# Neighbourhood attention in a hybrid encoder: full-height score passes, equal key chunks, V split once by key columns, heads' output split during the gates

## The chip, the cores and the metric

The kernel runs on one core of one Trainium2 chip. The metric is the device time of one execution in microseconds (us). Of the core's engines, PE is TensorE (PEld its weight loads), DVE is VectorE, ACT is ScalarE, POOL is GpSimd, and SP is SyncE, which here issues most DMAs.

## What is computed

One encoder layer on two sequences with shared weights: a sample of 512 tokens and a prompt of 1024, each with 16 meta tokens in front.

```
h = rmsnorm(x) * g_mix
q, k, v, u, gate_na, gate_fn = split(h @ w_in)
y_na = neighbourhood_attention(q, k, v) @ w_branch_na     # 8 heads of 64
y_fn = fourier_mix(u) @ w_branch_fn
x = x + (sigmoid(gate_na) * y_na + sigmoid(gate_fn) * y_fn) @ w_out
x = x + relu(rmsnorm(x) * g_mlp @ w_up) ** 2 @ w_down
```

and a final rmsnorm. The tokens form a grid of 64 columns. Each attends to 8 rows x 16 columns of the grid around it, with a bias by relative position, and to all meta tokens.

## The kernel before

Every float32 operand of a product is split into two parts of 12 bits, hi and lo, and hi.hi, hi.lo and lo.hi are summed in PSUM: three passes of PE. A split is an ACT copy (hi) and a subtraction (lo), on DVE out of PSUM (`split_ps`, L113) and on POOL out of SBUF (`split_sb`, L131, used by `weights`, L124). Weights stream through three kinds of tiles with two buffers each: raw, hi and lo.

The sequences go one after the other, the sample first. For each, `run` (L312) computes V (`project_v`, L274), then the attention (L429), the gates (L690), the product of the heads' output with its branch weights (`merge_na`, L712), the Fourier branch, the output projection and the MLP. A planner orders each engine's instructions by the trace of the program, by priority and by what is ready in its own model, so loads can be issued well ahead of their place in the program; what `behind` (L99) encloses stays behind marks on its engines. In a queue an instruction that waits holds up those after it.

**V.** A tile of 128 tokens is 24 matmuls, a DVE copy, and one DMA of 256 KB to a place `vd` in DRAM (L305). `spread_v` (L647) then copies V from DRAM to DRAM into the order of the key chunks, `vf` (L660), and the rests of chunks to `vp` (L674). For each head and block of query rows, `values` (L499) loads V from there and splits it: ACT L512 and POOL L513, for rests L519 and L520.

**Units.** A unit is 128 queries of a head: 8 rows by 16 columns of the grid. Four units (j = 0 to 3, for 24, 32, 32 and 24 key columns) make a block of 8 query rows; the sample has one such block for each head, the prompt two. So the sample has 32 units and the prompt 64. A unit has three stages:

- the scores: the queries' hi and lo stand in the two halves of a tile of 128 rows, and the keys' hi in both halves, so one pass (L549) gives hi.hi and lo.hi. A second one (L550) gives hi.lo from the 64 rows of the head. The bias is loaded by SP (L686). DVE adds it and takes the least (L554), ACT takes the exponential (L556), DVE the reciprocal (L557) and the product (L558).
- the transposes of the probabilities (L564), chunk by chunk, each split by ACT and DVE (L115, L116). A chunk is a whole number of key rows: 120, 128 or 96 keys, and in some blocks of 32 key columns a rest of 32 keys, which has splits of its own.
- the products with V (L585), two for each chunk, of 128 and 64 output columns.

After j = 3, ACT copies half of the sum (L589), DVE adds it to the other (L590), and ACT and POOL split the result into `oT` in SBUF (L593, L594), in the order of the tokens.

The stages of different units overlap by lags (L613). Between them PE gets steps of three matmuls (L444 to L446): the queries and keys of the next pair of heads (`project`, L450), early gates (L596), and in the sample a folding of weights (L217). The steps are dealt out so that they are used up after 5/6 of the units of a pair:

```
nxt = chain(project(pr + 1) if pr < 3 else after, islice(early, 8 * quota[pr]))
...
step(x, lambda s: feed(min(steps, (3 * u + s + 1) * steps * 6 // (3 * nu * 5))))
```

**Gates.** For each of eight blocks of 128 channels, one or two weight tiles of 512 KB are loaded, and 24 matmuls for each 512 tokens follow. Gates that were computed early come back from DRAM first (L695).

Of the kernel before, what the change touches and what calls it, by code (L numbers as in the profile page):

```python
# [33 lines left out]
KC0 = (0, 8, 24, 40)  # L34
QC, KCOL, VC, GNA, GFN = 0, 512, 1024, 2048, 3072
# [6 lines left out]
def row_blocks(rows):  # L42
    """How a block of 8 query rows meets its keys, for column blocks with 24 and with 32 key columns.

    Key slots: the meta tokens, the key rows, the meta tokens again. s0, n: first slot and number of
    slots; rpc, full: slots to a chunk and number of full chunks; meta: where the meta tokens are;
    row0: where key row 0 of the loads is; loads: (table, first of 8 reversed query rows, how many,
    first key row, how many, offset); masked: (first query, last, first slot, last) never loaded."""
    if rows == 8:
        loads = [("un", 0, 8, 0, 8, 7)]  # L50
        return [{24: dict(s0=0, n=10, rpc=5, full=2, meta=0, row0=1, loads=loads, masked=[(0, 128, 9, 10)]),
                 32: dict(s0=0, n=9, rpc=4, full=2, meta=0, row0=1, loads=loads, masked=[])}]
    first = [("un", 4, 4, 0, 8, 7), ("4", 0, 4, 0, 11, 7)]
    last = [("4", 4, 4, 0, 12, 3), ("un", 0, 4, 4, 8, 3)]
    b0 = dict(s0=0, n=12, rpc=4, full=3, meta=0, row0=1, loads=first, masked=[(64, 128, 9, 12)])
    return [{24: b0, 32: b0},
            {24: dict(s0=3, n=15, rpc=5, full=3, meta=14, row0=2, loads=last, masked=[(0, 128, 0, 2), (0, 64, 2, 6)]),
             32: dict(s0=5, n=13, rpc=4, full=3, meta=12, row0=0, loads=last, masked=[(0, 64, 0, 4)])}]


class Layer:
# [27 lines left out]
    def mark(self):  # L89
        """The last instruction so far of each engine that the weights pass."""  # L90
# [22 lines left out]
    def split_ps(self, ps, hi, lo, ref=None):  # L113
        """hi + lo = ps, exactly. ref: where hi is read, if not where it is written."""
# [3 lines left out]
    def wtile(self, kind, shape):  # L118
        """A tile of up to 1044 columns of the pool through which the weights stream."""
# [4 lines left out]
    def weights(self, src, to=None, scale=1.0, lo_engine=None):  # L124
        """One weight tile: DMA, then the exact split. to: the pair of tiles for it, if not of the streaming pool."""
# [25 lines left out]
    def norm(self, x, gain, out, n=128, junk=None):  # L151
        """out = rmsnorm(x) * gain for n tokens, one to a partition."""
# [5 lines left out]
        # y = (2 v) ** -0.5: a first guess, negative, from the bits, then Newton steps, each of which turns the sign  # L158
# [9 lines left out]
    def transpose_in(self, hn, hT, pos, n=128):  # L168
        """hT[:, kt, pos:pos+n] (hi and lo) = hn[:n].T, where hT is in one pair of tiles or in more"""
# [13 lines left out]
    def tables(self):  # L183
        """Tables of negated biases in DRAM: "un" has the column mask, "4" the row mask as well.

        The queries of a block lie in reverse order (last row first, last column first), so that
        the tables are read with positive strides."""
        nc, tc = self.nc, self.tc
        self.g = {(t, w): self.dram.tile([2, 16 * H, 15 * w], F32, name=f"g_{t}{w}") for t in ("un", "4") for w in (24, 32)}
        # negated meta biases, between masked columns  # L190
# [4 lines left out]
        with tc.tile_pool(name="tab", bufs=1, side="right", reuse_waits="tile") as p:  # L195
# [5 lines left out]
            for w in (24, 32):  # L201
                # blocks (0, 3) or (1, 2)
# [14 lines left out]
    def fold_u(self, p):  # L217
        """W_u times the channel DFT of its group: columns [256 cos | 4 nyquist | 252 sin], hi and lo, to DRAM."""
# [871 lines left out]
```

## Time and profile before

| | before |
|---|---|
| median of 3 runs (lowest to highest) | 2160.71 us (2157.1 to 2161.77) |
| span of the profiled execution | 2160.5 us |
| mean granted clock of PE | 0.984 |
| PE idle for DVE, ACT, POOL or DMA, longest single wait | 8.2 us, for DVE L166, at the start |

The profile is of one execution. Its span reaches from the first to the last instruction. A row of the timeline has the start (us from the span's start), the duration, the engine, the line of the kernel, the operation, the tile written, the tiles read, the shape, and how many instructions are merged in it. In brackets stands for how long the engine was idle before, and what ended that. Rows of the chain have start, length and what ran. Rows of a window have its length and then the busy time of each engine, the granted clock (1.00 is full), the mean busy share of the DMA engines and what they moved in GB/s.

### The profile page before, as it was taken

To read this page: it belongs to the slowest core of one execution; us is meant where nothing else is said; L and a number is where in the kernel's file an instruction comes from. 1 tells how busy PE (TensorE), PEld (TensorE's weight loads), DVE (VectorE), ACT (ScalarE), POOL (GpSimd) and SP (SyncE) were. 2 spreads that over 40 slices of the span, in tenths; PEclk is the share of its full clock that TensorE was granted. 3 is DMA by queue.
4 is the path that set the end of the run, shared out by engine and by line. 5 is a ranking of instruction groups with operands and counts; after the bars stand their busy time and mean duration, and the time that the engine had idled before them with its cause. 6 is when DMAs were issued, how large, how long until landed. Compare 5 with 4: busy or idle time off the path is not lost.

```text
span 2160.5 us, 26214 instructions
## 1 busy us (share of the span) xinstructions
PE 2100.4 (97%) x9947; PEld 1710.0 (79%) x9947; DVE 1072.0 (50%) x1937; ACT 699.4 (32%) x1321; POOL 700.7 (32%) x644
## 2 busy tenths in 40 slices
PE   6999999999999999999999999999999999999998
PEld 4877877878888788777788788788888888888886
DVE  6571155565664544565500627275445544454446
ACT  3673322433332315566532213132122112211221
POOL 3343545244444412444413624203122112221120
PEclk9999989999999999999989999999999999999999
DMA  6644543334323344333422253302112111121111
GB/s 201 192 143 152 141 132 100 92 108 126 114 82 103 110 158 148 102 101 85 127 78 59 60 162 105 136 10 78 39 49 62 46 40 45 54 59 39 39 40 78
DMA packets 232090, 205.01 MB, mean 95 GB/s; under 512 B 39982, under 2 KB 202542, under 8 KB 231790
## 3 DMA queue, kind: packets, MB, share of 16 engines
q1 hardware_dynamic: 219196, 187.97, 28.8%
q0 software_dynamic: 12768, 15.37, 2.9%
q8 instruction: 78, 1.28, 0.3%
q14 instruction: 48, 0.39, 0.1%
HBM read 184.29 MB, written 27.38 MB: 98 GB/s over the span
## 4 chain that ended last, share of the span: by engine, by line
PE 84%; DVE 8%; DMA 2%; issue 2%; ACT 2%; POOL 1%; POOLq 0%; SPq 0%; DVEq 0%; ACTq 0%
PE ps_o L111 23%; PE ps_s L111 23%; PE ps_mm L111 23%; PE ps_mm L444 3%; PE ps_mm L445 3%; PE ps_mm L446 3%; PE ps_o L585 2%; PE ps_t L564 1%; PE ps_s L550 1%; DVE s L756 1%; PE ps_t L176 1%; DVE hn L783 1%; DVE hn L166 1%; PE ps_s L549 1%; POOL hT L759 0%
## 5 line engine op out<-in xcount | busy, mean ns | idle before, releaser
L135 POOL TENSOR_TENSOR w_lo<-w_raw,w_hi 128x1024 fp32r<-128x1024 f32 x175 | 422.1, 2416 | 991.1 <-ACT w_hi L134 468.9
L957 DVE TENSOR_TENSOR relu<-relu 128x512 f32<-128x512 f32 (+1 forms) x98 | 204.1, 2083 | 357.9 <-ACT relu L956 357.9
L134 ACT CAST w_hi<-w_raw 128x1024 fp32r<-128x1024 f32 x176 | 182.9, 1048 | 361.2 <-DMA w_raw<-in_w_up 93.9
L444 PE MATMUL ps_mm<-hT,w_hi 128*128 128x512 f32 (+3 forms) x304 | 125.3, 412 | 1.7 <-DVE wu_lo L116 1.7
L111 PE MATMUL ps_s<-gate,w_hi 128*128 128x512 f32 (+1 forms) x528 | 126.9, 390 | 0.0
L111 PE MATMUL ps_mm<-gate,w_hi 128*128 128x512 f32 (+1 forms) x528 | 126.3, 388 | 0.2
L958 ACT CAST hid_hi<-relu 128x512 fp32r<-128x512 f32 (+1 forms) x98 | 60.0, 612 | 198.1 <-DVE relu L957 197.8
L111 PE MATMUL ps_o<-gate,w_hi 128*128 128x512 f32 (+1 forms) x512 | 122.8, 390 | 0.6 <-DVE gate L116 0.6
L111 PEld LDWEIGHTS ps_mm<-gate,w_hi 128*128 128x128 f32 x528 | 97.6, 188 | 23.1 <-DVE gate L116 0.8
L111 PEld LDWEIGHTS ps_s<-gate,w_hi 128*128 128x128 f32 x528 | 98.2, 188 | 22.2
L111 PEld LDWEIGHTS ps_o<-gate,w_hi 128*128 128x128 f32 x512 | 95.3, 188 | 22.8 <-DVE gate L116 0.9
L445 PE MATMUL ps_mm<-hT,w_hi 128*128 128x512 f32 (+3 forms) x304 | 108.9, 358 | 0.0
L446 PE MATMUL ps_mm<-hT,w_lo 128*128 128x512 f32 (+3 forms) x304 | 108.8, 358 | 0.0
L756 DVE TENSOR_TENSOR s<-s,s 128x384 f32<-128x384 f32 (+2 forms) x34 | 25.2, 778 | 163.2 <-POOL s L753 101.1
L984 DVE TENSOR_TENSOR acc<-acc,ps_o 128x512 f32<-128x512 f32 x120 | 81.8, 682 | 28.4 <-PE ps_o L111 28.4
L111 PE MATMUL ps_mm<-w_hi,hid_hi 128*128 128x512 f32 x240 | 94.0, 392 | 0.9 <-DVE acc L984 0.9
L959 DVE TENSOR_TENSOR hid_lo<-relu,hid_hi 128x512 fp32r<-128x512 f32 (+1 forms) x98 | 70.4, 718 | 48.0 <-ACT hid_hi L958 46.3
L984 DVE TENSOR_TENSOR acc<-acc,ps_s 128x512 f32<-128x512 f32 x120 | 81.8, 682 | 24.7 <-PE ps_s L111 24.7
L111 PE MATMUL ps_mm<-w_lo,hid_hi 128*128 128x512 f32 x240 | 93.5, 390 | 0.3 <-POOL w_lo L135 0.3
L984 DVE TENSOR_TENSOR acc<-acc,ps_mm 128x512 f32<-128x512 f32 x120 | 81.8, 682 | 24.2 <-PE ps_mm L111 24.1
L111 PE MATMUL ps_s<-w_hi,hid_hi 128*128 128x512 f32 x240 | 93.8, 391 | 0.0
L111 PE MATMUL ps_o<-w_hi,hid_hi 128*128 128x512 f32 x240 | 93.7, 391 | 0.0
(393 smaller groups left out, 4575.1 us busy)
## 6 DMA issues: line engine op xcount, KB each, us to landing
w_raw<-in_w_up SPq DMA_DIRECT2D x64, 512.0 KB
w_raw<-in_w_down SPq DMA_DIRECT2D x64, 512.0 KB
w_raw<-in_w_in SPq DMA_DIRECT2D x56, 512.0 KB
w_raw<-in_w_out SPq DMA_DIRECT2D x16, 512.0 KB
raw<-in_w_na SPq DMA_DIRECT2D x16, 256.0 KB
raw<-in_w_fnA SPq DMA_DIRECT2D x16, 256.0 KB
raw<-in_w_fnB SPq DMA_DIRECT2D x16, 256.0 KB
r<-in_x_prompt SPq DMA_DIRECT2D x8, 512.0 KB
```

The source lines that it names most:

```text
L111: self.nc.tensor.matmul(out, a, b, start=(i == 0), stop=(i == len(terms) - 1))
L134: nc.scalar.copy(out=hi, in_=raw)
L135: (lo_engine or nc.gpsimd).tensor_tensor(out=lo, in0=raw, in1=hi.bitcast(F32), op=ALU.subtract)
L444: nc.tensor.matmul(ps, a[0], b[0], start=(kt == 0), stop=False)
L445: nc.tensor.matmul(ps, a[0], b[1], start=False, stop=False)
L446: nc.tensor.matmul(ps, a[1], b[0], start=False, stop=(kt == 7))
L585: nc.tensor.matmul(po[:m, j * 128:(j + 1) * 128], v, x, start=(i == 0), stop=(i == len(ops) - 1))
L756: nc.vector.tensor_tensor(out=f[2 + i], in0=f[0], in1=f[1], op=(ALU.add, ALU.subtract)[i])
L957: nc.vector.tensor_tensor(out=r, in0=r, in1=r, op=ALU.mult)
L958: nc.scalar.copy(out=hi[:, cs], in_=r)
L959: nc.vector.tensor_tensor(out=lo[:, cs], in0=r, in1=hi[:, cs].bitcast(F32), op=ALU.subtract)
L984: nc.vector.tensor_tensor(out=acc[t][:, cs], in0=acc[t][:, cs], in1=ps, op=ALU.add)
```

## The change

- The lo of a head's keys is written to both halves of a tile of its own (`kl`, four buffers of one head instead of two of a pair). The second score pass goes over all 128 rows; it now adds lo.lo as well.
- A block's keys are the same slots for all its units: 9 slots in the sample, 12 and 13 in the prompt. They are cut into equal chunks: 2 x 108 and 3 x 96 keys in the sample, 3 x 96, 3 x 128, 3 x 104 and 4 x 104 in the prompt. No rests are left.
- V is split where it is computed, by ACT and DVE. Hi and lo go side by side to four places in DRAM, one for each block of key columns: eight DMAs for a tile of 128 tokens. `spread_v` goes. For each head and block of query rows, four DMAs bring hi and lo at once, in rows of 512 bytes, and nothing is split then.
- A head's output is put in the order of the tokens by DVE's addition and stored in DRAM (`od`). For each pair of heads it comes back through the weights' raw tiles and is split by ACT and POOL ahead of gate blocks 1 to 4. `oT` is allocated after the attention's pool is closed.

```diff
+KW = (24, 32, 32, 24)
+MPOS = (0, 16, 0, 8)
+VROW = H * 2 * DH
...
     if rows == 8:
-        loads = [("un", 0, 8, 0, 8, 7)]
-        return [{24: dict(s0=0, n=10, rpc=5, full=2, meta=0, row0=1, loads=loads, masked=[(0, 128, 9, 10)]),
-                 32: dict(s0=0, n=9, rpc=4, full=2, meta=0, row0=1, loads=loads, masked=[])}]
+        return [dict(s0=0, n=9, meta=0, row0=1, loads=[("un", 0, 8, 0, 8, 7)], masked=[])]
     first = [("un", 4, 4, 0, 8, 7), ("4", 0, 4, 0, 11, 7)]
     last = [("4", 4, 4, 0, 12, 3), ("un", 0, 4, 4, 8, 3)]
-    b0 = dict(s0=0, n=12, rpc=4, full=3, meta=0, row0=1, loads=first, masked=[(64, 128, 9, 12)])
-    return [{24: b0, 32: b0},
-            {24: dict(s0=3, n=15, rpc=5, full=3, meta=14, row0=2, loads=last, masked=[(0, 128, 0, 2), (0, 64, 2, 6)]),
-             32: dict(s0=5, n=13, rpc=4, full=3, meta=12, row0=0, loads=last, masked=[(0, 64, 0, 4)])}]
+    return [dict(s0=0, n=12, meta=0, row0=1, loads=first, masked=[(64, 128, 9, 12)]),
+            dict(s0=5, n=13, meta=12, row0=0, loads=last, masked=[(0, 64, 0, 4)])]
+def key_chunks(n):
+    c = -(-n // 128)
+    assert n % c == 0
+    return c, n // c
+def most_chunks(blocks):
+    return max(key_chunks(b["n"] * w)[0] for b in blocks for w in KW)
...
-        self.vd = self.dram.tile([128 + T, H, DH], F32, name=f"vd_{name}")
+        nslot = T // 64 + 2
+        most = most_chunks(row_blocks(T // 64))
+        self.vw = [self.dram.tile([nslot * w, VROW], F32, name=f"vw_{name}{j}") for j, w in enumerate(KW)]
         meta = self.meta_values
         if meta is not None:
-            for s in (0, 64 + T):
-                nc.sync.dma_start(self.vd[s:s + 64], meta)
-        self.meta_values = self.vd[0:64]
+            for j, w in enumerate(KW):
+                for s in (0, nslot - 1):
+                    nc.sync.dma_start(self.vw[j][s * w:(s + 1) * w], meta[j][0:w])
+        self.meta_values = self.vw
...
-            vs = p.tile([128, 512], F32R, name="pt0", tag="pt0", bufs=self.ptb).bitcast(F32)
-            nc.vector.tensor_copy(vs[:n], ps[:n])
-            vs = vs.rearrange("p (h d) -> p h d", h=H)
...
+            vs = p.tile([128, 4, most, 2 * DH], F32R, name="vb", tag="vb", bufs=2).rearrange("p j c x -> p (j c x)")
+            vs = vs[:, :VROW].rearrange("p (h i d) -> p h i d", h=H, i=2)
+            self.split_ps(ps[:n].rearrange("p (h d) -> p h d", h=H), vs[:n, :, 0], vs[:n, :, 1])
+            vs = vs.bitcast(F32).rearrange("p h i d -> p (h i d)")
+            for j, w in enumerate(KW):
+                if t < 0:
+                    at = self.vw[j][0, :]
+                    for m, c0 in ((16, MPOS[j]), (w - 16, 0 if MPOS[j] else 16)):
+                        nc.sync.dma_start(
+                            bass.AP(at.tensor, at.offset + c0 * VROW, [[VROW, m], [(nslot - 1) * w * VROW, 2], [1, VROW]]),
+                            vs[:m, None, :].to_broadcast([m, 2, VROW]))
+                else:
+                    for r in range(2):
+                        s = (1 + 2 * t + r) * w
+                        nc.sync.dma_start(self.vw[j][s:s + w], vs[r * 64 + KC0[j]:r * 64 + KC0[j] + w])
...
-            op, close_oT = self.open(f"oT_{name}", "left")
             with ExitStack() as fold:
                 after = self.fold_u(fold.enter_context(pool("fold", "right"))) if i == 0 else iter(())
-                oT = self.attention(att, op, name, T, hT, w0, after)
+                od = self.attention(att, name, T, hT, w0, after)
             close_att()
+            op, close_oT = self.open(f"oT_{name}", "left")
+            oT = [self.pair(op, [128, T], f"oT{pr}", 1) for pr in range(4)]
...
-            near_end = self.gates(T, hT, mixed, sig)
+            near_end = self.gates(T, hT, mixed, sig, lambda pr: self.weights(od[pr], oT[pr]))
...
-        oT = [[op.tile([128, T], F32R, name=f"oT{pr}{i}") for i in range(2)] for pr in range(4)]
+        most = most_chunks(blocks)
+        wide = max(b["n"] * w for b in blocks for w in KW)
+        od = [self.dram.tile([128, T], F32, name=f"o_{name}{pr}") for pr in range(4)]
...
-            kl = p.tile([128, nslot, 64], F32R, name="kl", bufs=2)
+            kl = [p.tile([128, nslot, 64], F32R, name="kl", bufs=4) for _ in range(2)]
...
-                    for hp in (own, slice(64 - 64 * hh, 128 - 64 * hh)):
+                    for hp in both:
...
-                    nc.vector.tensor_tensor(out=flat[2][own, gs], in0=src[:, m:], in1=flat[hh][own, gs].bitcast(F32),
-                                            op=ALU.subtract)
-                    if m:
-                        nc.vector.tensor_tensor(out=copies(kl, own), in0=src[:, None, None, :m].to_broadcast([64, 2, 3, 16]),
-                                                in1=copies(kh[hh], own).bitcast(F32), op=ALU.subtract)
+                    for hp in both:
+                        nc.vector.tensor_tensor(out=flat[2 + hh][hp, gs], in0=src[:, m:], in1=flat[hh][own, gs].bitcast(F32),
+                                                op=ALU.subtract)
+                        if m:
+                            nc.vector.tensor_tensor(out=copies(kl[hh], hp), in0=src[:, None, None, :m].to_broadcast([64, 2, 3, 16]),
+                                                    in1=copies(kh[hh], own).bitcast(F32), op=ALU.subtract)
...
-            nf = max(blk[w]["full"] for w in (24, 32))
-            vb = p.tile([128, 2, 2, nf, 2, DH], F32R, name="vb", tag="vb", bufs=2)
...
+            b = blocks[R]
+            vb = p.tile([128, 4, most, 2 * DH], F32R, name="vb", tag="vb", bufs=2)
+            for j, w in enumerate(KW):
+                nch, ck = key_chunks(b["n"] * w)
+                at = self.vw[j][0, :]
+                nc.sync.dma_start(vb[:ck, j, :nch].bitcast(F32),
+                                  bass.AP(at.tensor, at.offset + b["s0"] * w * VROW + h * 2 * DH,
+                                          [[VROW, ck], [ck * VROW, nch], [1, 2 * DH]]))
+            return vb
...
-            w = 24 if j in (0, 3) else 32
-            b = blk[w]
-            n, rpc, full, ck = b["n"], b["rpc"], b["full"], b["rpc"] * w
+            w = KW[j]
+            b = blk
+            n = b["n"]
             W = n * w
+            nch, ck = key_chunks(W)
...
-            nc.tensor.matmul(ps[:, :W], qs[hh][own, qc], kl[own, kw[0], kw[1]], start=False, stop=True)
+            nc.tensor.matmul(ps[:, :W], qs[hh][:, qc], kl[hh][:, kw[0], kw[1]], start=False, stop=True)
...
-            nch = full + (1 if n > full * rpc else 0)
             for c in range(nch):
-                k0, k1 = c * ck, min((c + 1) * ck, W)
-                nc.tensor.transpose(tp[:k1 - k0, c * 128:(c + 1) * 128], sc[:, k0:k1], self.ident)
+                nc.tensor.transpose(tp[:ck, c * 128:(c + 1) * 128], sc[:, c * ck:(c + 1) * ck], self.ident)
             pt = [p.tile([128, 512], F32R, name=f"pt{i}", bufs=self.ptb) for i in range(2)]
-            nf = full * 128
-            self.split_ps(tp[:ck, :nf], pt[0][:ck, :nf], pt[1][:ck, :nf])
-            if nch > full:
-                self.split_ps(tp[:32, nf:nf + 128], pt[0][:32, nf:nf + 128], pt[1][:32, nf:nf + 128])
+            self.split_ps(tp[:ck, :nch * 128], pt[0][:ck, :nch * 128], pt[1][:ck, :nch * 128])
...
-                k = ck if c < full else 32
-                v = (vb[:ck, (w == 32), j // 2, c] if c < full else vp[:, j // 2]).rearrange("p i d -> p (i d)")
-                ops.append((128, v, pt[0][:k, cs]))
-                ops.append((64, v[:, :64], pt[1][:k, cs]))
+                v = vb[:ck, j, c]
+                ops.append((128, v, pt[0][:ck, cs]))
+                ops.append((64, v[:, :64], pt[1][:ck, cs]))
...
-                ot = p.tile([128, 512], F32, name="ot", tag="ot", bufs=1)[own]
-                nc.scalar.copy(out=ot, in_=po[64:])
-                nc.vector.tensor_tensor(out=ot, in0=po[:64], in1=ot, op=ALU.add)
-                hi, lo = (t[own, R * 512:(R + 1) * 512].rearrange("p (i j a) -> p j i a", j=4, a=16) for t in oT[pr])
-                ov = ot.rearrange("p (j i a) -> p j i a", j=4, a=16)[:, :, ::-1, ::-1]
-                nc.scalar.copy(out=hi, in_=ov)
-                nc.gpsimd.tensor_tensor(out=lo, in0=ov, in1=hi.bitcast(F32), op=ALU.subtract)
+                half = p.tile([128, 512], F32, name="ot", tag="ot", bufs=1)[own]
+                ot = p.tile([128, 512], F32, name="os", bufs=2)[own]
+                nc.scalar.copy(out=half, in_=po[64:])
+                nc.vector.tensor_tensor(out=ot.rearrange("p (i j a) -> p j i a", j=4, a=16)[:, :, ::-1, ::-1],
+                                        in0=po[:64].rearrange("p (j i a) -> p j i a", j=4, a=16),
+                                        in1=half.rearrange("p (j i a) -> p j i a", j=4, a=16), op=ALU.add)
+                nc.sync.dma_start(od[pr][own, R * 512:(R + 1) * 512], ot)
...
-        self.spread_v(name, blocks)
...
-    def spread_v(self, name, blocks):
-        nc = self.nc
-        self.vfull, self.vpart = {}, {}
...
+        *sigs, bring = sigs
...
         for dm in range(8):
+            if dm in (1, 2, 3, 4):
+                bring(dm - 1)
             for sig, c0 in zip(sigs, (GNA, GFN)):

```

More of the change, by code (lines that the diff above doesn't have):

```diff
@@ L427, in new_hT, with attention @@
         return [tuple(pool.tile([128, 8, T + extra], F32R, name=f"hT{i}") for i in range(2))]
-    def attention(self, p, op, name, T, hT, w0, after):
+    def attention(self, p, name, T, hT, w0, after):
         hT, = hT
@@ L471, in project @@
                 gs = slice(t0, t0 + cn - m)
-                flat = [t.rearrange("p s c -> p (s c)") for t in kh + [kl]]
+                flat = [t.rearrange("p s c -> p (s c)") for t in kh + kl]
                 for hh in range(2):
                     own = slice(64 * hh, 64 * hh + 64)
+                    both = own, slice(64 - 64 * hh, 128 - 64 * hh)
                     src = ps[own, :cn]
-                    for hp in (own, slice(64 - 64 * hh, 128 - 64 * hh)):
+                    for hp in both:
                         nc.scalar.copy(out=flat[hh][hp, gs], in_=src[:, m:])
@@ L541, in unit @@
             qs, kh, kl = state[pr]
-            own = slice(64 * hh, 64 * hh + 64)
-            bm = p.tile([128, 416], F32, name="bm", bufs=8 if T == 512 else 4)
+            bm = p.tile([128, wide], F32, name="bm", bufs=8 if T == 512 else 4)
             self.bias(bm, h, j, w, b)
@@ L573, in unit @@
             po = shared["o"]
[L574 removed]
+            vb = shared["v"]
             ops = []
```

60 lines of the change are left out of this document (3 added, 57 removed).

## The prediction

> **What bounds the kernel now.** I read the page first, then the busy times by stage, then the timeline of TensorE (PE), then the rows of its waits.
>
> ```profile
> PE 2100.4 (97%) x9947; PEld 1710.0 (79%) x9947; DVE 1072.0 (50%) x1937; ACT 699.4 (32%) x1321; POOL 700.7 (32%) x644
> PE 84%; DVE 8%; DMA 2%; issue 2%; ACT 2%; POOL 1%; POOLq 0%; SPq 0%; DVEq 0%; ACTq 0%
> ```
>
> PE is busy for 2100.4 of 2160.5 us and carries 84% of the chain that ended last. So the change is worth what it takes from PE's own time, plus or minus idle time. It works in the two attention stages:
>
> ```profile
> 70.00:177.70 107.70, 98.07 (x589) 79.02 (x589) 72.61 (x235) 74.68 (x225) 44.79 (x84) 0.96 0.49 141
> 811.00:1088.00 277.00, 274.92 (x1523) 220.78 (x1522) 152.52 (x403) 161.16 (x386) 106.50 (x218) 0.97 0.39 110
> ```
>
> (Columns: window, length, busy PE, PEld, DVE, ACT, POOL, clock, DMA share, GB/s.) In the prompt's attention PE idles 2 us of 277: time taken from PE there is gained. The sample's has 10 us of idle, and DVE and ACT are busy for 70% of it.
>
> The end of a matmul row is modelled, so I price a pass by the distance from its start to the start of the next. One unit (128 queries of a head) in the prompt:
>
> ```profile
> 950.39 0.62 PE L585 MATMUL ps_o<-pt,vb 120*128 120x128 f32 x6
> 950.85 0.45 PE L444 MATMUL ps_mm<-hT,w_hi 128*128 128x512 f32 x1
> 951.14 0.40 PE L445 MATMUL ps_mm<-hT,w_hi 128*128 128x512 f32 x1
> ...
> 951.60 0.29 PE L549 MATMUL ps_s<-kh,q 128*128 128x288 f32 x1
> 951.83 0.40 PE L550 MATMUL ps_s<-kl,q 64*128 64x288 f32 x1
> 952.15 0.50 PE L444 MATMUL ps_mm<-hT,w_hi 128*128 128x512 f32 x1
> 952.50 0.39 PE L445 MATMUL ps_mm<-hT,w_hi 128*128 128x512 f32 x1
> 952.73 0.39 PE L446 MATMUL ps_mm<-hT,w_lo 128*128 128x512 f32 x1
> ```
>
> and passes of full height among their like:
>
> ```profile
> 101.82 0.29 PE L444 MATMUL ps_mm<-hT,w_hi 128*128 128x264 f32 x1
> 101.94 0.28 PE L445 MATMUL ps_mm<-hT,w_hi 128*128 128x264 f32 x1
> 965.50 0.33 PE L445 MATMUL ps_mm<-hT,w_hi 128*128 128x352 f32 x1
> 965.67 0.32 PE L446 MATMUL ps_mm<-hT,w_lo 128*128 128x352 f32 x1
> ```
>
> **Term 1, the second score pass.** L549 to L550 takes 0.23 us, L550 to the next 0.32, and that one 0.35: 0.90. Among full-height passes 264 columns take 0.12 and 352 take 0.17, so 288 take 0.13; 512 take 0.23 (952.50 to 952.73). Two score passes and their follower without the 64-row neighbour: 0.13 + 0.13 + 0.23 = 0.49. The 64-row pass thus costs 0.41 a unit, on both its sides. The new pass has 128 rows (the keys' lo in both halves) and the same columns: 96 units x 0.41 = 39.4 us of PE. It could be nothing, if the place and not the height made these gaps (rival E), and not much more. The Trainium skill (TensorEngine Tiling (Array Packing), Key Properties) says that a change of tiling mode drains TensorE, which is this step; it gives no figure, and the trace agrees with the 0.23 and 0.32 above.
>
> **Term 2, the 32-row value passes.** Units with 32 key columns in the sample, and in the prompt's second row block, end with a short chunk:
>
> ```profile
> 87.06 0.45 PE L585 MATMUL ps_o<-pt,vb 128*128 128x128 f32 x4
> 87.44 0.38 PE L585 MATMUL ps_o<-pt,vp 32*64 32x128 f32 x2
> 87.75 0.50 PE L444 MATMUL ps_mm<-hT,w_hi 128*128 128x512 f32 x1
> 88.08 0.39 PE L445 MATMUL ps_mm<-hT,w_hi 128*128 128x512 f32 x1
> ```
>
> 0.38 + 0.31 + 0.33 = 1.02, where six even passes and their follower take 0.46 + 0.29 = 0.75 (950.39 to 951.14). Equal chunks (3 x 96; 4 x 104) keep the number of passes: 32 units x 0.27 = 8.6 us.
>
> **Term 3, columns.** Blocks of 24 key columns lose 24 columns in the sample (240 to 216) and 48 in the prompt's second block (360 to 312): 16 units each, two passes, at 0.05 us for 88 columns: 1.3 us. Sum of the three: 49 us.
>
> **What of it lands.** From 5/6 of each pair's units on (L640) no projection lies between the units. There DVE's loop of reduce, wait for ACT's exponential, reciprocal, multiply sets the pace:
>
> ```profile
> 961.23 0.58 DVE L554 CUSTOM_DVE_ANT_0 sc<-ps_s,bm 128x416 f32<-128x416 f32 x1
> 963.18 0.58 DVE L554 CUSTOM_DVE_ANT_0 sc<-ps_s,bm 128x416 f32<-128x416 f32 x1
> 965.12 0.53 DVE L554 CUSTOM_DVE_ANT_0 sc<-ps_s,bm 128x360 f32<-128x360 f32 x1
> ```
>
> 1.95 us a unit. By 1/6 these are 16 of 96 units; I count their gain, 0.41 and a third of 0.27, half: 4 us are lost (bounds 0 and 8). In the sample PE falls from 98.07 by 13.1 + 4.3 + 0.3 to about 80, near DVE's 72.61; I take 3 us lost (0 to 8).
>
> **V.** The splits that go were these, on ACT and POOL:
>
> ```profile
> L512 ACT CAST vb<-vr x48: 399/510/518, 75.8 to 1069.1; 128x384 fp32r<-128x384 f32 x16, 120x256 fp32r<-120x256 f32 x8, 128x256 fp32r<-128x256 f32 x8, 96x384 fp32r<-96x384 f32 x8
> L513 POOL TENSOR_TENSOR vb<-vr,vb x48: 724/1008/1119, 76.3 to 1071.0; 128x384 fp32r<-128x384 f32 x16, 120x256 fp32r<-120x256 f32 x8, 128x256 fp32r<-128x256 f32 x8, 96x384 fp32r<-96x384 f32 x8
> ```
>
> 24 us of ACT and 48 of POOL, beside PE except once:
>
> ```profile
> 60.88 9.16 DMA vf_sample<-vd_sample
> 70.09 5.72 DMA vr<-vf_sample
> 75.83 0.41 ACT vb L512
> 77.42 0.76 PE L564 MATMUL ps_t<-ident,sc 128*128 128x128 f32 x3 [1.39 <-DVE sc L558]
> 77.40:82.00 4.60, 4.58 (x17) 3.75 (x18) 2.71 (x11) 4.25 (x15) 1.95 (x5) 0.63 0.79 200
> ```
>
> V's copies between DRAM places end at 70.0, its load at 75.8, and ACT stands at V's split with the first exponential behind it. PE idles 1.39 us, and the next 4.6 us go at a mean clock of 0.63, which costs 4.6 x 0.37 = 1.7 us. Afterwards no ACT work waits for V, and nothing copies it between DRAM places: a gain of 3 us (0 to 3). V's loads, issued where the old one was (70.1), are first used four units later (L613), some 10 us, against the 5.72 above.
>
> What is added: each tile of V (24 matmuls of 0.23: 5.5 us of PE) is split by ACT and DVE and stored by eight DMAs instead of one. On SP the row below prices the issue, so 3 us a tile: it fits, with the score biases queued behind it, which have four or eight buffers. The lo of the keys is written twice: DVE again, 40 x 0.5 and 16 x 0.25, is 24 us over both stages, beside PE; the separate splits of short chunks go from DVE.
>
> ```profile
> L305 SPq DMA_DIRECT2D vd_prompt<-pt x8: 320/379/571, 779.2 to 816.1; - x8
> L480 DVE TENSOR_TENSOR kl<-ps_mm,kh x34: 401/500/520, 63.8 to 989.7; 64x344 fp32r<-64x344 f32 x12, 64x264 fp32r<-64x264 f32 x8, 64x336 fp32r<-64x336 f32 x8, 64x248 fp32r<-64x248 f32 x6
> 1069.74 0.38 SPq L128 DMA_DIRECT2D w_raw<-in_w_in  x1
> ...
> 1072.09 20.86 SPq L695 DMA_DIRECT2D gate<-gate_prompt x6
> ```
>
> **The heads' output.** The new store of a head's block waits on SP for DVE, with biases and, at the end of attention, the gates' loads behind it. SP already stands for 20.86 us at that place, up to 1093, five us past the end of attention (1088), and the first weights had been issued ahead of it (1069.74). Four loads and splits move into the gates, through the two raw buffers of the weights. In the prompt a weight lasts 48 matmuls, 11 us: hidden. In the sample 24, 5.5 us:
>
> ```profile
> 216.07 1.05 ACT L134 CAST w_hi<-w_raw 128x1024 fp32r<-128x1024 f32 x1 [3.17 <-PE ps_o L111]
> 218.00 2.39 POOL L135 TENSOR_TENSOR w_lo<-w_raw,w_hi 128x1024 fp32r<-128x1024 f32 x1 [3.19 <-PE ps_o L111]
> DMA to landing us min/median/max: 4.0/4.1/4.2
> ```
>
> A raw buffer serves a tile in 4.1 + 1.05 + 2.4 = 7.6 us, half a tile in less; three tiles for every two weights on two buffers need 7.4 us each on average. Each split now waits 3.2 us for PE to free its place; that is the slack, and 0.2 us a tile too little takes some of it over ten tiles. I take 2 us for this and POOL's later work (0 to 8).
>
> **The sum.** -49 + 4 + 3 - 3 + 2 = -43: 2160.5 - 43 is 2117.5, and with the 0.2 us by which the median of the runs (2160.71) lies above the span, 2118. Own range 2109 to 2127.
>
> **Rivals.**
> A, other engines become the bound: only the prompt's units before the 5/6 pay (53 x 0.41 + 16 x 0.27 = 26): 2135. For it: DVE's and ACT's 70% in the sample. Against it: 3.06 us of PE a unit (98.07 / 32), 2.5 afterwards, still above the loop's 1.95. Chance 0.17.
> B, all 49 land, and the last stretch of the prompt's attention keeps its clock:
>
> ```profile
> 1070.57 0.54 PE L585 MATMUL ps_o<-pt,vb 96*64 96x128 f32 x4 [1.26 <-DVE pt L116]
> 1072.00:1074.00 2.00, 2.00 (x11) 1.78 (x10) 1.76 (x5) 1.53 (x4) 0.43 (x4) 0.50 1.09 223
> 1090.00:1092.00 2.00, 2.00 (x8) 1.58 (x7) 0.00 (x0) 1.99 (x2) 1.19 (x1) 0.66 0.00 0
> ```
>
> After an idle 1.26 us PE ran at 0.50 from 1071 to 1091; with DVE's loop as the bound six units would save about 5. With the stall: -57, 2104. Chance 0.10.
> C, the gaps of a faster PE drop the clock at the seven other ends of pairs: three units of 1.95 and some 3.5 us until it is back (as after 77.4), at half speed, cost about 4 us each: 28 back, 2146. Chance 0.07. The Trainium skill (TensorE: Matmul & The Clock Gate, Part 1) wants a whole idle window of about 3.4 us before half speed; by that rule C cannot come. The trace disagrees: 1.26 us were enough.
> D, slower: V's transfers come late. A row block of the sample brings 9 x 112 rows of 512 B, 516 KB, and has four units (10 us) to hide in. It decides if they take longer; at the rate of the 5.72 us row (120 KB) they take 24.6, 14.6 late, eight times: 117 us, 2235. Against it: 512 KB of weights land in 4.1. Chance 0.04.
> E, the gaps are not the height's: only terms 2 and 3, 2151, and the 8 us of the gates may take most of that back. Chance 0.04.
>
> **Numbers.** Forecast 0.58. Below 2101 and above 2139 lie C, D, E and the edges of A and B: about 0.2. A measurement here tells apart about 0.2% (4 us). Faster by more: all but D and half of E, 0.94; same 0.02; slower 0.04.
>
> **What would show it.** L549 to L550 at 0.11 to 0.19, and the follower of L550 at its usual distance; no 32-row passes; the first transposes of the sample without idle before them; PE's attention windows at about 80 and 244 us; gates of the sample without waits for the splits of weights. Wrong would be: gaps of 0.3 after a 128-row L550; clock 0.50 at ends of pairs; PE waiting for the load of V.

## The result and the profile after

The changed kernel takes 2179.84 us (median of 4 runs, 2177.13 to 2184.93), the kernel before 2161.24 (2157.1 to 2167.01) beside it: a ratio of 1.0083, 95% interval 1.0059 to 1.0108. It was forecast at 2118 and is slower by 19 us. The profiled execution's span is 2175.9 us. Times are medians of executions in the chip's faster state; one of e11's below, 2302.86 us, was in a slower one and is left out.

The busy times and the chain of the page after:

```profile
PE 2068.4 (95%) x9947; PEld 1710.2 (79%) x9947; DVE 1082.3 (50%) x1960; ACT 669.0 (31%) x1222; POOL 634.8 (29%) x548
PE 80%; DVE 9%; DMA 3%; issue 3%; ACT 3%; POOL 2%; SPq 1%; POOLq 0%; DVEq 0%; ACTq 0%
```

PE has 32 us less to do (2100.4 before), and yet the span is longer by 15.4: idle time grew from 60.1 to 107.5. The score passes themselves came out as priced. A unit of the prompt, in the timeline after:

```profile
856.90 0.29 PE L558 MATMUL ps_s<-kh,q 128*128 128x288 f32 x1
857.03 0.29 PE L559 MATMUL ps_s<-kl,q 128*128 128x288 f32 x1
857.17 0.33 PE L464 MATMUL ps_mm<-hT,w_hi 128*128 128x352 f32 x1
857.33 0.32 PE L465 MATMUL ps_mm<-hT,w_lo 128*128 128x352 f32 x1
```

These are 0.13, 0.14 and 0.16 us from start to start, where 0.23, 0.32 and 0.35 stood (there with a follower of 512 columns). So the loss is elsewhere. The attention windows, from 70 to the sample's first gate group and from 33 us after the start of the prompt's V to the prompt's first gate group, say where. Before (the sample's row stands in the prediction) and after, with the columns of the prediction:

```profile
800.00:1087.80 287.80, 285.72 (x1571) 229.58 (x1570) 153.90 (x405) 161.97 (x385) 106.50 (x218) 0.97 0.39 114
```
```profile
70.00:196.90 126.90, 89.56 (x587) 80.66 (x587) 75.43 (x239) 64.14 (x181) 23.45 (x49) 0.84 0.65 190
818.00:1102.70 284.70, 265.44 (x1571) 231.38 (x1570) 160.93 (x422) 135.60 (x318) 51.55 (x151) 0.95 0.46 129
```

The sample's attention grew from 107.7 to 126.9 us, with 37 us of idle PE; the prompt's fell by 3.1 though PE has 20 less to do. What lies between the two kept its length: from the sample's first gate group to the prompt's V 589.6 us passed before (177.69 to 767.30) and 588.4 after (196.95 to 785.32). Both losses lie at the starts, and SP's queue shows them (start, time from the first to the last of the merged issues, waits included, what):

```profile
40.92 7.82 SPq L315 DMA_DIRECT2D vw_sample<-vb  x8
48.84 42.94 SPq L321 DMA_DIRECT2D vw_sample<-vb  x32
92.29 1.36 SPq L527 DMA_DIRECT2D vb<-vw_sample  x3
...
800.88 81.11 SPq L321 DMA_DIRECT2D vw_prompt<-vb  x64
882.09 1.89 SPq L527 DMA_DIRECT2D vb<-vw_prompt  x4
```

V's stores hold SP for 43 and 81 us, and V's first load, biases and weights stand behind them. Most of that is waiting for V's splits, whose second half is DVE's (SP's waits in the sample's start, 38 to 100, and in the prompt's, 785 to 890: us, times, longest):

```profile
SPq L321 <- DVE vb L126: 27.1, 2, 16.2
```
```profile
SPq L321 <- DVE vb L126: 52.2, 5, 26.1
```

Why the splits are late is in ACT's timeline; ACT makes the hi parts. First a row of the chain (start, length), V's last product of the sample on PE, then ACT's rows (the last one from the prompt):

```profile
50.28 5.57 PE ps_s L121 x24
```
```profile
41.28 0.59 ACT L125 CAST vb<-ps_s 128x512 fp32r<-128x512 f32 x1 [1.90 <-PE ps_s L121]
58.79 0.36 ACT L497 CAST kh<-ps_o 64x248 fp32r<-64x248 f32 x1 [16.93 <-PE ps_o L465]
...
69.24 0.59 ACT L125 CAST vb<-ps_o 128x512 fp32r<-128x512 f32 x1
...
83.36 0.58 ACT L125 CAST vb<-ps_mm 128x512 fp32r<-128x512 f32 x1
83.84 0.59 ACT L125 CAST vb<-ps_s 128x512 fp32r<-128x512 f32 x1
...
807.82 0.59 ACT L125 CAST vb<-ps_mm 128x512 fp32r<-128x512 f32 x1 [10.86 <-DMA vw_prompt<-vb]
```

PE had all of the sample's V by 55.9, but the last three tiles are split at 69, 83 and 84, behind the copies of keys and queries. V's tiles have two places (the tiles of V's chunks), each free only when its eight stores have landed: the last row shows ACT idle for 10.86 us until such stores end. The planner laid the later splits behind other work. PE pays for it:

```profile
85.62 0.61 PE L558 MATMUL ps_s<-kh,q 128*128 128x288 f32 x1 [4.77 <-DVE vb L126]
...
95.11 0.87 PE L588 MATMUL ps_o<-pt,vb 108*128 108x128 f32 x4 [8.64 <-DMA vb<-vw_sample]
...
885.24 1.84 PE L588 MATMUL ps_o<-pt,vb 96*128 96x128 f32 x12 [4.45 <-DMA vb<-vw_prompt]
```
```profile
885.00:895.00 10.00, 6.62 (x30) 0.53 0.55 149
895.00:905.00 10.00, 8.59 (x36) 0.50 0.69 180
905.00:915.00 10.00, 9.63 (x37) 0.78 0.63 171
```

(The second fence: window, busy PE, clock, DMA share, GB/s.) After the wait of 4.45 us for the load PE runs at about half clock for some 20 us. By these three rows (busy time times what the clock lacks: 3.1, 4.3 and 2.1) an estimate of 9.5 us more is lost in that way.

### The profile page after: what moved, and what is told of

The parts are those of the page before. It is cut to its first block, busy times and chain, and to the rows that moved or that the text cites. A ratio compares the mean times of both kernels' runs of the same rounds, so it can differ in the third digit from the quotient of the medians.

```text
span 2175.9 us, 26228 instructions
## 1 busy us (share of the span) xinstructions
PE 2068.4 (95%) x9947; PEld 1710.2 (79%) x9947; DVE 1082.3 (50%) x1960; ACT 669.0 (31%) x1222; POOL 634.8 (29%) x548
## 4 chain that ended last, share of the span: by engine, by line
PE 80%; DVE 9%; DMA 3%; issue 3%; ACT 3%; POOL 2%; SPq 1%; POOLq 0%; DVEq 0%; ACTq 0%
PE ps_o L121 23%; PE ps_s L121 22%; PE ps_mm L121 22%; PE ps_mm L463 3%; PE ps_mm L465 2%; PE ps_mm L464 2%; PE ps_o L588 1%; DVE s L732 1%; PE ps_t L186 1%; PE ps_t L571 1%; DVE hn L176 1%; DVE hn L759 1%; DMA bm<-g_un 1%; DVE raw L748 1%; DMA sin<-in_sin_prompt 1%
```

## Experiments

Theory P (places): two places make the splits and stores late. Rivals: S, only the queue (SP held by the stores); Q, the transfers are late by themselves; D, VectorE binds (this D is not the prediction's). After the first runs theory O came in: one queue, and the order of all engines laid out around its lateness. Times are medians in us; before took 2159 to 2163 beside them. The runs that the argument rests on, with the two attention windows (bounds as above, each from one execution; for e1 and e6 from the chain's gate and V groups):

| | V's places, stores' queue | us | sample | prompt |
|---|---|---|---|---|
| before | | 2161.24 | 107.7 | 287.8 |
| after | two, SP | 2179.84 | 126.9 | 284.7 |
| e1 | for all, SP | 2151.27 | 105.0 | 280.2 |
| e6 | for all, ACT | 2149.83 | 112.2 | 268.9 |
| e9 | for all, SP in the sample, ACT in the prompt | 2141.45 | 106.2 | 268.9 |
| e17 | no stores | 2128.84 | 97.0 | 264.9 |
| e18 | no stores, 64-row pass | 2148.29 | 100.0 | 281.8 |

**Places for V's tiles** (e1):

```diff
-            vs = p.tile([128, 4, most, 2 * DH], F32R, name="vb", tag="vb", bufs=2)...
+            vs = places(t).rearrange("p (h i d) -> p h i d", h=H, i=2)
...
+                    self.project_v(name, T, hT, att, self.wv, lambda t: p.tile(    # the sample
+                        [128, D], F32, name=("hn", "xt")[t in (0, 2, 3)], bufs=(2, 3)[t in (0, 2, 3)]).bitcast(F32R))
...
+                    if t in (0, 1, 6, 7):    # the prompt
+                        return att.tile([128, 4, 4, 2 * DH], F32R, name="vb", tag="vb", bufs=2)...
+                    return att.tile([128, T // 64 + 2, 64], F32R, name="kl", bufs=4)...
```

> The changed kernel, but V's tiles get places of their own: in the sample the five tiles of the reading pool (whose contents are read by then), in the prompt the two of V's chunks and the four of the keys' lo. Theory P (places): in the changed kernel V's tiles have two places, each free only when eight stores have landed, so the later splits stand on ACT and DVE behind the copies of keys and queries, and the stores that wait for them hold up SP's queue with biases, weights and V's loads in it. By the profile of the changed kernel the start of attention lost some 22 us of idle TensorE and 5 us of lowered clock in the sample (windows 70 to 110) and some 20 us of both in the prompt (865 to 915). With places for all, nearly all of it goes: 2180 - 44 = 2136 us, range 2126 to 2146; the stores are all issued before the first load of V, and TensorE waits less than 2 us for V's loads. Rival Q (transfers): the stores of V and the loads that wait for the last of them are late by themselves (64 stores in the prompt, 40 in the sample, of 2 KB and more a row); then more places move little: 2165 to 2180, with TensorE still waiting 4 us and more for V's load. Rival D (VectorE): the keys' second copies bind DVE at the start; then the waits for DVE stay (kl, biased scores) and the time is 2155 to 2165.

It took 2151.27, ratio to before 0.9949 (0.9933 to 0.9964). That is outside P's range, but 29 of the 44 us, so P is a good part of it; Q had given 2165 to 2180, and PE no longer waits for V's loads. The sample's gates began at 175.0 (after: 196.95). But the stores, now in time, still filled SP up to 65.1 in the sample, and a stall stayed at the start of the prompt. SP's rows, then one of PE:

```profile
57.86 7.26 SPq L320 DMA_DIRECT2D vw_sample<-xt  x16
66.69 1.95 SPq L533 DMA_DIRECT2D vb<-vw_sample  x4
```
```profile
844.36 0.62 PE L469 MATMUL ps_mm<-hT,w_hi 128*128 128x344 f32 x1 [5.55 <-DVE kl L510]
```

**Another queue, two places** (e2 on GpSimd's, e5 on ScalarE's):

```diff
-                        nc.sync.dma_start(self.vw[j][s:s + w], ...)
+                        nc.gpsimd.dma_start(self.vw[j][s:s + w], ...)    # e5: nc.scalar
```

> The changed kernel, but V's stores go out from GpSimd's queue instead of SyncE's; two places as in the changed kernel. Theory P: SP's queue is free, so biases and weights come early and the first scores wait less; but the splits of V still stand behind the keys' copies, so the last store and V's first load stay about as late, and the stores now hold up GpSimd's zeros and weight splits: some 5 to 20 us gained, 2160 to 2175. If SP's blocked queue alone were the cause (rival S), this alone would give back some 40 us: 2135 to 2145. Rival Q (transfers): 2175 to 2185.

> The changed kernel with its two places, but V's stores go out from ScalarE's queue, right behind ScalarE's own half of the split. The run with places gave 2151 and kept a stall at the start of the prompt's attention: between the first four units and the others TensorE's order has 72 passes of the next pair's projection in a row, and 840 to 890 lost some 18 us of idle and clock there. Theory O (one queue and the order made for it): the 64 stores, the biases and V's loads share SyncE's queue, so the loads come late, and the order of all engines is laid out around that lateness: projections first, bare units afterwards. With the stores on another queue that empties as V is split, the units stand between the projections again: 2135 us, range 2125 to 2150, though only two places are there. Rival P (places alone): two places keep the splits late whatever the queue; like the stores on GpSimd's queue it stays at 2170 to 2185.

They took 2180.65 and 2164.58. In e2 a free SP queue alone gains nothing (S falls): the stores of the sample's third tile of 128 tokens waited for its split until 71, and PE waited 14.4 us for V's load. The time lies above P's range and in the one given for Q. On ScalarE's queue the stores stand right behind ScalarE's own splits; the second and third tiles were split at 52.4 and 57.7, where the kernel after has 69.2 and 83.4, and with two places e5 gained 15 us, half of what e1 did. Early splits alone don't explain it: e2 split them at 54.2 and 69.3, also earlier than the kernel after, and gained nothing. So it is neither P alone nor O as it was put.

**Both** (e6, e9; e9 takes SP's queue in the sample and ScalarE's in the prompt):

```diff
+                        (nc.sync if meta is None else nc.scalar).dma_start(self.vw[j][s:s + w], ...)
```

> Places for all of V's tiles, as in the run with places, and the stores on ScalarE's queue. Theory O: from 2151 the 18 us of the prompt's start go, and some 6 of the 10 that the sample's start still loses (windows 70 to 100): 2127 us, range 2120 to 2138; the prompt's windows from 840 on run at clock 1.00. Rival A (VectorE and ScalarE bind at the starts, not queue or order): no more than 5 us under the run with places, 2146 to 2155.

> Places for all; V's stores on SyncE's queue in the sample and on ScalarE's in the prompt. The two runs with places both took 2150, but from different stages: with the stores on SyncE's queue the sample's gates began at 175.0 and V plus attention of the prompt took 313.2 us; on ScalarE's queue 182.2 and 301.9. If the stages add, this takes the better of each: 2147 - 7 = 2140 us, range 2135 to 2145. If ScalarE's queue gained in the prompt only because the sample had been later (rival), it stays at 2150.

They took 2149.83 and 2141.45; e9's ratio to before is 0.9898 (0.9879 to 0.9916), as expected. e6 missed: the prompt's start was mended (V and attention 301.9 us, 313.2 in e1), but in the sample ScalarE stood in issuing, with the keys' copies behind it, and the gates began at 182.2:

```profile
59.40 16.61 ACTq L320 DMA_DIRECT2D vw_sample<-xt  x16
76.05 0.36 ACT L503 CAST kh<-ps_o 64x248 fp32r<-64x248 f32 x1 [19.81 <-DMA vw_sample<-xt]
```

The stages add, as e9 shows. What changed at the prompt's start is seen in the order of PE's instructions in the traces (p projection passes, S a unit's two score passes, T transposes, V products with V, with their numbers; from the prompt's first projection):

```
before     p120 S p15 S p18 S p6 T3 p12 S p6 T3 p3 V6 p6 S p6 T3 p6 V6 p6 S ...
after      p139 S p4 S p10 S p6 T3 p9 T3 p14 S p58 V12 S S T6 V10 S V2 S T3 V2 S ...
e1         p144 S p9 S p1 S p14 T3 S T3 p72 V12 S S T6 V10 S V2 S T3 V2 S ...
e9         p125 S p11 S p17 S p6 T3 p9 S T3 V6 S T1 p24 T2 p6 V6 p6 S p6 T3 ...
no stores  p120 S p15 S p18 S p6 T3 p9 S T3 V1 p12 V5 p6 S p6 T3 p6 V6 p6 S ...
```

In after and e1 the projections are spent first (58 and 72 in a row) and the units come bare afterwards; in e9 and without stores they mostly alternate with the units, as before. Theory O reads this so: the planner's model has V's load late and lays out other work first. No run changed the order alone, so this is argued and not shown.

**Small things** (e8, e10 to e12): the second lo copy of the keys by GpSimd from SBUF; the sample's meta tokens stored to the first slot alone (nothing reads its last slot).

```diff
-                nc.vector.tensor_tensor(out=flat[2 + hh][hp, gs], in0=src[:, m:], ...)       # second half
+                nc.gpsimd.tensor_copy(flat[2 + hh][hp, gs], flat[2 + hh][own, gs])           # e8, e12
-                bass.AP(at.tensor, at.offset + c0 * VROW, [[VROW, m], [(nslot - 1) * w * VROW, 2], [1, VROW]])
+                bass.AP(at.tensor, at.offset + c0 * VROW, [[VROW, m], [1, VROW]])            # e10 to e12
```

> As the run with places and stores on ScalarE's queue, but the second copy of the keys' lo is made by GpSimd from the first copy in SBUF instead of by VectorE from PSUM. If VectorE binds the sample's attention (it was busy for 7.5 to 9 of 10 us in its windows, and TensorE waited 5.5 and 3 us for kl), this gives 3 to 8 us more: 2121. Rival: VectorE's copies are hidden and GpSimd's are slower and later than what they replace: no change or up to 5 us slower.

> As the mixed run, and the sample's meta tokens are stored to the first slot alone (its last slot is read by nobody: the prompt copies the first). Theory T (transfers): in the sample V's stores are bound by the DMA engines, which from 44 to 52 moved 98 and 80 GB/s for the meta stores at a share of 0.95 and 0.72 and afterwards 3.6 MB of V at some 240 GB/s, to 84. Half of the meta stores (0.46 MB at 98 GB/s, 4.7 us) less brings all that follows forward: 3 to 5 us less than the mixed run, 2136. Rival (order and queue, not transfers): no change.

> Stores on ScalarE's queue in both sequences, with the sample's meta tokens stored once. Its order of TensorE's work is the even one in the sample too, but ScalarE itself stood from 59.4 to 76 in issuing 16 stores. Theory T: the stores can't be issued faster than the DMA engines take them, so the half meta store gives 3 to 5 us here too, from 2150 to 2146. Rival (an even order is what counts): then the first sixteen stores, which were held up by the meta stores, are early enough and most of ScalarE's 16 us stand goes: 2138.

> As the mixed run with one meta store, and the keys' second lo copy by GpSimd. By the run with that copy on GpSimd (2149 against 2150) it changes nothing: 2136, as its pair. In its order the prompt's first units stand as in the kernel before; if that counts, up to 5 us less: 2131.

e8 took 2148.68 (e6 2149.83), e10 2142.65 (e9 2141.45), e11 2143.33 (e6 2149.83) and e12 2139.85. VectorE's second copies of the keys don't bind (D falls as far as they go). Fewer meta stores help only where ScalarE issues: its stand of 16.61 us became 10.94. e12 is the fastest of the kernels that compute all of the layer, 0.9895 of before (0.9875 to 0.9916); from e9 it can't be told apart.

**The second score pass over 64 rows again** (e3 after, e4 on e1, e7 on e6):

```diff
-            nc.tensor.matmul(ps[:, :W], qs[hh][:, qc], kl[hh][:, kw[0], kw[1]], start=False, stop=True)
+            nc.tensor.matmul(ps[:, :W], qs[hh][64 * hh:64 * hh + 64, qc], kl[hh][64 * hh:64 * hh + 64, kw[0], kw[1]], start=False, stop=True)
```

> The changed kernel, but the second score pass again goes over the 64 rows of its head alone (the lo of the keys is still written to both halves). It leaves out only the product of the two lo parts, as the kernel before did. Term 1 of the prediction: 0.41 us a unit, 96 units, 39 us of TensorE; in the units that wait for V or VectorE it costs nothing, so I expect 30 us more: 2210, range 2200 to 2220. Rival (the gaps were not the height's): no change, 2175 to 2185.

> Both edits: places for all tiles of V, and the second score pass over 64 rows. If term 1 is worth what the prediction said and the start stalls are gone, it stands 35 us (28 to 42) above the run with places alone: 2171. If the sample's attention is then bound by VectorE and not by TensorE, it is less: 15 to 25 us.

> As the run with places and stores on ScalarE's queue, with the second score pass over 64 rows: term 1 by itself, without a stall around it. Prediction: 39 us of TensorE of which 4 + 3 don't land, so 32 us above its pair: 2159 if that is 2127. By the two runs before with places it was 25 us (2176 against 2151) with stalls, so 25 to 35.

They took 2198.05, 2175.98 and 2170.75: 18, 25 and 21 us above their pairs. The pass is worth much (the prediction's rival E falls), but less than the 32 us that it was to give.

**V's transfers taken out.** Loads from a small tensor that doesn't depend on the stores (e16), and besides no stores at all (e17), and that with 64 rows (e18). These kernels leave out V's own values in the attention. Here `dummy` has 128 rows, from V's first tile. In e13 to e15, the same three kernels, every partition read one and the same row; those took 2369.59, 2324.64 and 2322.73, bound by these loads: they tell of that alone (last section).

```diff
-                at = self.vw[j][0, :]
+                at = self.dummy[0, :]
...
-                                          [[VROW, ck], [ck * VROW, nch], [1, 2 * DH]]))
+                                          [[VROW, ck], [0, nch], [1, 2 * DH]]))
```

> As the run before it, and V isn't stored at all (it is still computed and split; the stores and the copies of the meta tokens' rows are left out). This is the world of the prediction, in which V's stores cost nothing: if its other terms hold, 2118 (2112 to 2126), with the sample's attention ending near 160 and not 174. If the other terms are too big (rival: the score pass is worth 20 and the sample is bound by other engines), 2128 to 2138.

> As the mixed run (2141), but the loads of V's chunks read a small tensor of 128 rows, stored once from V's first tile, with the packets and bytes of the real loads. The attention weighs the wrong values; all of V's stores stay. If the wait for the last store is what the starts still lose, 2130; if queue, bytes and the order laid out around them, 2141. I expect 2138. If loads from few places are slow by themselves even with 128 rows, it is above 2150 and tells nothing.

> As the run before it, without V's stores and without the copies of the meta tokens' rows. The world of the prediction, in which V's stores cost nothing: 2118 (2112 to 2126) if its other terms hold, with the sample's attention ending near 160. If the other terms are too big (the score pass worth 20 to 25 in place of 32, the sample bound by waits on other engines), 2126 to 2136.

> As the run without V's stores, with the second score pass over 64 rows: 39 us of TensorE by the prediction, 32 of them landing; by the three pairs so far 18, 25 and 21. I expect 25 us above its pair; 32 if the stalls had hidden part of it.

They took 2141.91, 2128.84 and 2148.29. e16 equals e9, so it isn't the wait for the last store that costs the rest. Without stores 12.6 us more are gained; e17 stands at 0.9858 of before (0.9837 to 0.9879), in the range for "the other terms are too big". The 64-row pass costs 19.5 us, where 25 were expected. The pages of e17 and e18, busy times:

```profile
PE 2049.2 (96%) x9947; PEld 1696.4 (80%) x9947; DVE 1080.8 (51%) x1960; ACT 668.6 (31%) x1222; POOL 633.5 (30%) x548
```
```profile
PE 2088.4 (97%) x9947; PEld 1704.1 (79%) x9947; DVE 1083.2 (51%) x1960; ACT 669.8 (31%) x1222; POOL 633.6 (30%) x548
```

39.2 us of PE hang on the 96 second passes: 0.41 each. (A little of it may be clock: 0.991 was granted in e17, 0.986 in e18.) The rows of one unit of the same form in e17 and in e18 say about the same, 0.49 against 0.88 from the first start to the last:

```profile
871.20 0.29 PE L566 MATMUL ps_s<-kh,q 128*128 128x288 f32 x1
871.33 0.29 PE L567 MATMUL ps_s<-kl,q 128*128 128x288 f32 x1
871.46 0.39 PE L472 MATMUL ps_mm<-hT,w_hi 128*128 128x512 f32 x1
871.69 0.39 PE L473 MATMUL ps_mm<-hT,w_hi 128*128 128x512 f32 x1
```
```profile
879.01 0.29 PE L566 MATMUL ps_s<-kh,q 128*128 128x288 f32 x1
879.23 0.40 PE L567 MATMUL ps_s<-kl,q 64*128 64x288 f32 x1
879.56 0.50 PE L472 MATMUL ps_mm<-hT,w_hi 128*128 128x512 f32 x1
879.89 0.40 PE L473 MATMUL ps_mm<-hT,w_hi 128*128 128x512 f32 x1
```

In the attention windows, e9, e17 and e18:

```profile
70.00:176.20 106.20, 85.84 (x590) 78.17 (x590) 73.97 (x236) 62.92 (x180) 23.64 (x49) 0.91 0.67 194
799.00:1067.90 268.90, 256.67 (x1571) 226.01 (x1571) 160.15 (x421) 134.83 (x317) 53.06 (x159) 0.98 0.49 138
```
```profile
70.00:167.00 97.00, 80.85 (x584) 73.31 (x583) 72.11 (x236) 61.89 (x179) 22.98 (x46) 0.96 0.54 158
788.10:1053.00 264.90, 255.47 (x1570) 225.28 (x1568) 162.49 (x421) 134.66 (x317) 51.22 (x153) 0.98 0.45 123
```
```profile
70.00:170.00 100.00, 92.53 (x584) 77.11 (x584) 72.44 (x236) 61.86 (x178) 22.73 (x46) 0.95 0.53 154
792.10:1073.90 281.80, 279.65 (x1570) 226.18 (x1569) 162.77 (x421) 135.95 (x317) 51.38 (x153) 0.98 0.42 116
```

From e18 to e17 the sample's PE falls by 11.7 us and its window by 3.0; the prompt's by 24.2 and 16.9. What PE no longer does in the sample becomes waits for DVE: all of PE's listed waits in these windows are for DVE, 16.1 us in e17 and 7.1 in e18. Two of the rows of each (us, times, longest):

```profile
PE ps_mm L238 <- DVE wu_lo L126: 6.0, 5, 2.5
PE ps_t L579 <- DVE pt L126: 3.3, 1, 3.3
```
```profile
PE ps_mm L238 <- DVE wu_lo L126: 3.0, 3, 1.8
PE ps_t L579 <- DVE pt L126: 0.9, 1, 0.9
```

## Why the prediction was wrong

**The step that failed** is "What is added" under V: "On SP the row below prices the issue, so 3 us a tile: it fits, with the score biases queued behind it". It took 0.38 us of issue for the price of a store. Left out were the place that the tile holds until its stores have landed, the queue that stands while a store waits for its split, and the bytes (4 x 128 KB + 4 x 96 KB a tile, 896 KB where one store had 256). V's stores cost 51 us (2179.84 to e17's 2128.84; by e16, the changed loads alone gain nothing). Places for all tiles give back 29 of them (e1), the other queue in the prompt 10 more (e9), and 12.6 stay.

The Trainium skill (Perfetto Trace Analysis, Per-instruction lifecycle) says that of a DMA the whole movement of data lies outside the window that its slice shows. The traces agree: before, a weight's issue takes 0.38 us on SP and its data have landed 4.1 us after its start (rows in the prediction). Nor is the row what the issuing engine pays: the sample's last 16 stores took SP 7.26 us in e1, and the same 16 held ScalarE for 16.61 in e6.

"V's loads, issued where the old one was (70.1), are first used four units later (L613), some 10 us" failed with that step: they were issued at 92.3, and PE stood for the 8.64 us up to 95.11.

The prediction's rival D named the place, V's transfers, but it priced the loads (117 us) and not the stores ahead of them, and had a chance of 0.04. The sign that the prediction gave, PE waiting for V's load, is in the profile with 8.64 and 4.45 us. Other waits at the two starts and the half clock after the second came on top (rows above); how the 51 us divide among them was not measured.

**Term 1** was sized right: 39.4 us forecast, 39.2 measured on PE, and the passes as forecast. **All three terms** on PE: in e17 the attention windows hold 80.85 and 255.47 us where before had 98.07 and 285.72: 47.5 less, and 49 was the sum. Terms 2 and 3 were not tested singly; e18, which has both but keeps the 64-row pass, has 11.6 us less than before in these windows, where they were priced at 9.9.

**What of it lands** was taken too well; this is the second step that failed, a term that was mis-sized. The forecast had 49 - 4 - 3 + 3 = 45 us for the two attention stages. In e17, where V's stores cost nothing, the windows are shorter by 10.7 and 22.9: 33.6. So without any cost of the stores the kernel takes 2128.84 and not 2118. The score pass by itself lands with 3.0 of its 11.7 us in the sample, where 13.1 - 3 were hoped for, and with 16.9 of 24.2 in the prompt, where 26.2 - 4 were. Rival A (only the prompt pays, 26 us: 2135) comes nearer to e17 than the forecast does: DVE's 72 us in a window of 97 bind in some stretches, as the 16.1 us of waits for it show, though not on average. In e8 taking DVE's second copies of the keys away moved nothing. Rival C did not come: over e17's execution 0.991 of the clock was granted, and 0.984 before. (By its own rows it should have been priced at 4.7 us an end, half of 3 x 1.95 + 3.5, and not 4.)

**The gates** cost nothing that these runs show (2 us were taken): the stretch from the sample's gates to the prompt's V takes 588.4 us, 589.6 before, and from the prompt's gates to the end it takes 1073 in both. That PE bounds most of the kernel held too (80% of the chain after); what was read wrongly, off a queue's issue times, is the cover of the new transfers.

**Open:** which of the stores' bytes, their queue and the order laid out for them costs e9's remaining 12.6 us. e16 excludes only the wait for the last store; e10 found nothing in 0.46 MB less. Why two places do better on ScalarE's queue than on GpSimd's is open as well.

## What to carry to other kernels

Price an added store by what it holds until it has landed (the tile's place, the queue, the bytes against what the DMA engines move in that stretch), not by its issue row. Where a planner lays out the order, a late load may move everything: compare the orders of before and after first. And a gain on the bounding engine lands only where the next engine has room; count it stage by stage.

## What the runs showed of the hardware

An engine that issues DMAs can stand far longer than the rows of single issues say. The 32 stores in the prompt of e9 on ScalarE's queue that go out from the tiles of V's chunks (duration in ns: least, median, greatest):

```profile
L320 ACTq DMA_DIRECT2D vw_prompt<-vb x32: 296/379/586, 780.6 to 823.1; - x32
```

That is 0.38 us each, but in the sample 16 of them took 16.61 us in e6 and 8 took 10.93 in e5, with ScalarE's work behind them. The DMA engines were 0.77 busy on average in that stretch of e6 (59.4 to 76); what made ScalarE stand was not tested. Loads in which all partitions read one row of 512 B were slow here: with 128 different rows in its place, and nothing else in the loads changed, the kernel went from 2324.64 (e14) to 2128.84 (e17). The DMA engines in the window 100 to 140, e14 and e17:

```profile
DMA packets 6486, 4.07 MB, mean 102 GB/s; under 512 B 305, under 2 KB 6306, under 8 KB 6482
```
```profile
DMA packets 10339, 6.38 MB, mean 160 GB/s; under 512 B 456, under 2 KB 9868, under 8 KB 10337
```
